# Head norm of a hybrid decoder layer: partner sums by a product with a 0/1 matrix

## The chip, the cores and the metric

The kernel runs on one core of a Trainium2 chip. The metric is the device time of one execution in microseconds (us), the median of several runs. A profile is one further execution, recorded instruction by instruction. The engines are named as the profile names them: PE is the tensor engine's matmul, PEld its weight load, DVE the vector engine, ACT the scalar engine, POOL is GpSimd, SP issues most of the DMAs.

## The reference, cut to what matters

One decoder layer over 1024 tokens and 1024 features. The input is normalised and projected to a short gated convolution group (512 columns) and to a stick-breaking attention group (8 heads of 64). Each group's output is then normalised per head of 64 features, both are joined and projected, and an MLP, a gated embedding and a last norm follow.

```python
def head_rmsnorm(y, g):
    b, s, w = y.shape
    yf = y.astype(jnp.float32).reshape(b, s, w // HEAD_DIM, HEAD_DIM)      # HEAD_DIM = 64
    yf = yf * lax.rsqrt(jnp.mean(yf * yf, axis=-1, keepdims=True) + EPS)
    return (yf.reshape(b, s, w) * g.astype(jnp.float32)).astype(y.dtype)
...
conv_out = head_rmsnorm(short_gated_conv(cb, cc, cu, conv_w[i]), g_conv_out[i])
attn = head_rmsnorm(attn.transpose(0, 2, 1, 3).reshape(b, s, W_ATTN), g_attn_out[i])
h = h + jnp.concatenate([conv_out, attn], axis=-1) @ w_out[i]
```

## The kernel before

Features lie on the 128 partitions and tokens along the free dimension, so a tile of the head norm holds two heads of 64 partitions over 1024 tokens. There are eight such tiles: four of the convolution (numbers 0 to 3, one per `conv_tile`) and four of the attention (4 to 7, one per pair of heads). A tile is worked in halves of 512 tokens.

For one half `head_norm` takes the squares on ACT (line 486), transposes them in 32x32 blocks on DVE (487) and sums 32 features at a time (489). That leaves `hpart`, 128 partitions by 16: partition quadrant q holds the sums of feature block q. A head is two neighbouring blocks, so four small copies bring each quadrant the sums of its neighbour (493), one operation adds them and the epsilon (495), and POOL raises the 16 columns to the power -0.5 (497). One slot later DVE spreads the result back over the features by another transpose (500) and multiplies the half by it and by the gain (501).

Projections, convolution and attention run interleaved between about 105 and 457 us. The order on PE there is written out by hand; the other engines' orders are planned by the scheduler from a simulated timeline. `attention_slots` counts slots. In a slot PE gets, in this order: the value products of an older chunk (`back_values`, line 645, tile `ps_av`), the transposes of a younger one (`back_transposes`, line 615, into a bank of tag `tr`), then whatever deferred work is due (`run_deferred`), then the score products of a new piece (line 586, tile `ps_z`), and last eight or so products of the projections as filler (line 158, tile `ps_mm`), taken from `fillers`. The transposed banks are emptied by an ACT copy (620) and a DVE subtraction (621); the value products use the result two slots after the transposes. Tag `tr` has two banks, taken in turn.

`head_norm` is a generator that is handed to `defer`. It starts at once; a `yield n` puts the rest off by n slots:

```python
def defer(g):
    deferred.append([slot[0] + next(g), g])
...
            elif hd == 1 and c == 1:
                defer(head_norm(y, G_ATTN + pr, 4 + pr, (0,)))
```

A convolution tile is handed over with both halves, `(0, 1)`, at the end of `conv_tile`; an attention tile half by half, as its value products end (c is the chunk of 256 tokens, hd the head). Until now no part of `head_norm` runs on PE. The squares and transposes live in a unit of group `C`, of which there are two; `conv_tile` holds one of them for its first products.

`normed` collects the finished tiles; `out_first` and the output projection's second half need them.

Of the kernel before, what the change touches and what calls it, by code (L numbers as in the profile page):

```python
# [9 lines left out]
F32 = mybir.dt.float32  # L10
F32R = mybir.dt.float32r
AF = mybir.ActivationFunctionType
ALU = mybir.AluOpType

P = 128
S = 1024
D = 1024
KT = D // P
HB = 512
NH = S // HB  # L20
EPS = 1e-6
LAG = 2
LAG_V = 2
LAG_S = 1
LAG_N = 2
QUOTA = 8.0
QUOTA_LAST = 7.4
N_WARM = 10
# [33 lines left out]
def hybrid_layer_kernel(ctx: ExitStack, tc: tile.TileContext, x, p, g_mix, w_in, conv_w, g_conv_out,  # L62
                        g_attn_out, w_out, g_mlp, w_up, w_down, g_ple, w_ple_gate, w_ple_proj,
                        g_final, out):
    nc = tc.nc
    x, p, w_in, conv_w, w_out, w_up, w_down, w_gate, w_proj, out = (
        x[0], p[0, 0], w_in[0], conv_w[0], w_out[0], w_up[0], w_down[0], w_ple_gate[0], w_ple_proj[0], out[0])

    const = ctx.enter_context(tc.tile_pool(name="const", bufs=1))
    small = ctx.enter_context(tc.tile_pool(name="small", bufs=4))  # L70
# [3 lines left out]
    U = Units(upool, {"A": 16, "VY": 10, "QK": 9, "T": 9, "W": 5, "C": 2, "E": 3})  # L74
    PS_BUFS = {"mm": 2, "z": 2, "tr": 2, "av": 2}

    def bank(tag):
        return psum.tile([P, HB], F32, name="ps_" + tag, tag=tag, bufs=PS_BUFS[tag])

    ident = const.tile([P, P], F32, name="ident")  # L80
# [10 lines left out]
                            base=0, channel_multiplier=-1)  # L91
    mhalf = const.tile([P, 16], F32, name="mhalf")
    nc.vector.memset(mhalf, -0.5)

    G_CONV, G_ATTN, CW = 0, 4, 8
    gc = const.tile([P, 20], F32, name="gc")
# [48 lines left out]
    def act_units(group):  # L145
        hi = [U.get(group, F32R, (P, 2, HB)) for _ in range(4)]
        lo = [U.get(group, F32R, (P, 2, HB)) for _ in range(4)]
        return hi, lo
# [184 lines left out]
    a, b = act_units("A")  # L333
# [12 lines left out]
    for k in range(4):  # L346
        a, b = U.get("T", F32R, (P, 2, HB)), U.get("W", F32R, (P, 2, HB))
# [47 lines left out]
    class Stream:  # L395
# [17 lines left out]
        def next(self):  # L413
            self._split()
            return self.ready.popleft()
# [59 lines left out]
    def head_norm(y, gcol, which, halves):  # L475

        for h in halves:  # L480
            while not U.free_q["C"]:
                yield 1
            sl = slice(h * HB, (h + 1) * HB)
            su = U.get("C", F32)
            sq, sqT = su[0][:, 0:HB], su[0][:, HB:S]
            nc.scalar.activation(sq, y[:, sl], AF.Square, scale=0.125)
            nc.vector.transpose(sqT, sq)
            part = small.tile([P, 16], F32, name="hpart")
            nc.vector.reduce_sum(out=part, in_=sqT.rearrange("p (b j) -> p b j", j=32), axis=mybir.AxisListType.X)
            other = small.tile([P, 16], F32, name="hother")  # L490
            for q in range(4):
                o = q ^ 1
                nc.vector.tensor_copy(out=other[32 * q:32 * q + 32], in_=part[32 * o:32 * o + 32])
            ms = small.tile([P, 16], F32, name="hms")
            nc.vector.scalar_tensor_tensor(out=ms, in0=part, scalar=EPS, in1=other, op0=ALU.add, op1=ALU.add)
            rs = small.tile([P, 16], F32, name="hrs")
            nc.gpsimd.tensor_tensor(out=rs, in0=ms, in1=mhalf, op=ALU.pow)
            if LAG_S:
                yield LAG_S
            nc.vector.transpose(sq, rs.unsqueeze(2).broadcast_to([P, 16, 32]))  # L500
            nc.vector.scalar_tensor_tensor(out=y[:, sl], in0=y[:, sl], scalar=gc[:, gcol:gcol + 1], in1=sq,  # L501
                                           op0=ALU.mult, op1=ALU.mult)
            U.put(su)
        yield LAG_N
        if halves[-1] == NH - 1:
            normed.add(which)

    def conv_tile(j, between=None):
# [29 lines left out]
        for h in range(NH):  # L538
# [4 lines left out]
            if h == 0 and between:  # L543
                between()
        stream.done(w2)
        defer(head_norm(y[0], G_CONV + j, j, (0, 1)))


# [6 lines left out]
    def run_deferred(everything=False):  # L555
        for d in list(deferred):
            while d in deferred and (everything or d[0] <= slot[0]):
                due = next(d[1], None)
                if due is None:
                    deferred.remove(d)  # L560
                else:
                    d[0] = slot[0] + due
# [64 lines left out]
    def back_values(ch, jp, aT2):  # L627
# [20 lines left out]
        if diag:  # L648
            y = Y[4 + pr][0]
            own = slice(hd * 64, hd * 64 + 64)  # L650
            oth = slice(64 - hd * 64, 128 - hd * 64)
            yc = y[own, c * 256:(c + 1) * 256]
            nc.scalar.copy(out=yc, in_=av[oth])
            nc.vector.tensor_tensor(out=yc, in0=av[own], in1=yc, op=ALU.add)
            if hd == 1 and c == 3:
                for u in V[pr]:
                    U.put(u)
                defer(head_norm(y, G_ATTN + pr, 4 + pr, (1,)))
            elif hd == 1 and c == 1:
                defer(head_norm(y, G_ATTN + pr, 4 + pr, (0,)))  # L660
# [4 lines left out]
    def attention_slots():  # L665

        def fronts():
            for pr in range(4):  # L670
                while pr not in qk_ready:
                    yield -1
                for hd in range(2):
                    for c in range(4):
                        ch = {"pr": pr, "hd": hd, "c": c}
                        for views, units in attend_front(pr, hd, c):
                            ch["views"], ch["units"] = views, units
                            yield pr
                        for jp in range(c + 1):
                            backq.append((slot[0] + LAG, ch, jp))  # L680
                    Q, K = QK[pr]
                    U.put(Q[hd])
                    for u in K[hd]:
                        U.put(u)

        fr = fronts()
        live = True
        while live or backq or pend:
            slot[0] += 1
            narrow = iter(())  # L690
            while pend and pend[0][0] <= slot[0]:
                for _ in narrow:
                    pass
                narrow = back_values(*pend.popleft()[1:])
                next(narrow, None)
            if backq and backq[0][0] <= slot[0]:
                _, ch, jp = backq.popleft()
                pend.append((slot[0] + LAG_V, ch, jp, back_transposes(ch, jp, narrow)))
            for _ in narrow:
                pass  # L700
            run_deferred()
            if live and len(U.free_q["T"]) >= 3:
                live = next(fr, None) is not None
            yield
# [72 lines left out]
    with tc.manual_schedule(engines={mybir.EngineType.PE}):  # L777
# [4 lines left out]
        for _ in attention_slots():  # L782
            credit += QUOTA if len(normed) < 6 else QUOTA_LAST
            while credit > 0:
                n = next(fill, None)
# [9 lines left out]
        for n in fill:  # L795
            slot[0] += (n or 3) / QUOTA
            run_deferred()
# [515 lines left out]
    with tc.manual_schedule(engines={mybir.EngineType.PE, mybir.EngineType.DVE, mybir.EngineType.Activation,  # L1313
# [107 lines left out]
        n = NP_ - 1  # L1421
# [231 lines left out]
```

## Time and profile before

| what | value |
|---|---|
| median of 3 runs | 1263.84 us (1262.51 to 1264.11) |
| profiled execution, its own time | 1267.23 us |
| span of the profile, first to last instruction | 1265.5 us |
| busy: PE / PEld | 1213.4 / 1004.0 us |
| busy: DVE / ACT / POOL | 963.0 / 628.5 / 236.4 us |
| mean granted TensorE clock | 0.986 of full speed |

Busy time is the sum of an engine's instructions. Matmuls are pipelined and their ends are modelled, so PE at 96% of the span is close to always occupied, but that alone does not say that it runs at its peak. The shares are means over stages with different limits; the head norm lies in one of them only, the stage from about 140 to 470 us.

### The profile page before, as it was taken

The numbers are of one execution on the slowest core, as the hardware profiler recorded it, in microseconds if no ns is written. First come the engines' busy times: TensorE is split into PE (matmuls) and PEld (weight loads), VectorE is DVE, ScalarE is ACT, GpSimd is POOL, SyncE is SP. The second block draws the span as 40 slices with busy tenths as digits, with TensorE's granted clock in tenths as the row PEclk, the third lists the DMA queues.
The fourth block names the chain that finished last, engine by engine and source line by source line (L and its number), as shares of the span: only waits on it lengthen the run. The fifth ranks groups of instructions, "written<-read, shape, count | busy, mean of one in ns | idle before, by whom it ended". The sixth has DMA issues, their size and how long they took to land.

```text
span 1265.5 us, 15613 instructions
## 1 busy us (share of the span) xinstructions
PE 1213.4 (96%) x5629; PEld 1004.0 (79%) x5629; DVE 963.0 (76%) x1367; ACT 628.5 (50%) x1049; POOL 236.4 (19%) x248
## 2 busy tenths in 40 slices
PE   8999999999998999899999999987899999999997
PEld 6788888878877788678888888865788888887786
DVE  3656898989989976678666766665889888886774
ACT  5445465555565432456545545563344444435543
POOL 3302544545448531000000000000000000002121
PEclk9999999999998999899999999989999999999899
DMA  9711011111122325124677776799787876567432
GB/s 361 221 34 44 28 31 34 35 34 34 34 67 89 128 81 203 66 92 164 231 271 251 262 276 249 276 302 325 243 258 228 264 239 214 190 207 229 134 101 99
DMA packets 152229, 209.71 MB, mean 166 GB/s; under 512 B 8004, under 2 KB 111448, under 8 KB 152152
## 3 DMA queue, kind: packets, MB, share of 16 engines
q1 hardware_dynamic: 151608, 207.67, 49.0%
q8 instruction: 44, 0.72, 0.2%
q10 hardware_dynamic: 544, 1.05, 0.2%
q14 instruction: 33, 0.27, 0.1%
HBM read 141.58 MB, written 67.11 MB: 165 GB/s over the span
## 4 chain that ended last, share of the span: by engine, by line
PE 51%; DVE 4%; DMA 3%; ACT 1%; issue 1%; SPq 0%; POOL 0%; POOLq 0%; DVEq 0%; ACTq 0%
PE ps_mm L1016 13%; PE ps_z L1016 12%; PE ps_av L1016 12%; PE ps_tr L1016 7%; PE ps_z L158 2%; PE ps_tr L158 2%; PE ps_mm L158 2%; PE ps_av L158 2%; DMA u<-hs_d 1%; DMA u<-h_d 1%; DVE u L1279 1%; DVE u L908 1%; DVE u L839 1%; DMA n_d<-u 1%; DVE u L842 1%
## 5 line engine op out<-in xcount | busy, mean ns | idle before, releaser
L158 PE MATMUL ps_mm<-u,u 128*128 128x512 f32 (+1 forms) x1464 | 366.4, 396 | 7.1 <-ACT u L904 2.6
L158 PEld LDWEIGHTS ps_mm<-u,u 128*128 128x128 f32 x1464 | 269.8, 190 | 62.3 <-ACT u L904 3.0
L908 DVE TENSOR_TENSOR u<-u,u 128x1024 fp32r<-128x1024 f32 (+2 forms) x214 | 231.2, 1101 | 43.1 <-ACT u L904 36.4
L904 ACT CAST u<-u 128x1024 fp32r<-128x1024 f32 (+2 forms) x214 | 195.0, 952 | 91.3 <-DVE u L842 20.4
L1016 PE MATMUL ps_z<-u,u 128*128 128x512 f32 x768 | 194.5, 396 | 14.4 <-DVE u L908 6.5
L1016 PE MATMUL ps_mm<-u,u 128*128 128x512 f32 x768 | 191.4, 391 | 6.5 <-DVE u L839 5.8
L1016 PE MATMUL ps_av<-u,u 128*128 128x512 f32 x744 | 186.1, 392 | 1.4 <-DVE u L908 1.4
L1016 PEld LDWEIGHTS ps_z<-u,u 128*128 128x128 f32 x768 | 145.9, 191 | 48.5 <-DVE u L908 8.3
L1016 PEld LDWEIGHTS ps_mm<-u,u 128*128 128x128 f32 x768 | 144.6, 189 | 38.2 <-DVE u L839 7.1
L1016 PEld LDWEIGHTS ps_av<-u,u 128*128 128x128 f32 x744 | 140.3, 189 | 31.8 <-DVE u L908 2.1
L123 POOL TENSOR_SCALAR me<-ms 128x1 f32<-128x1 f32 x24 | 10.3, 430 | 705.0 <-DVE u L839 619.6
L839 DVE TENSOR_TENSOR u<-ps_av,u 128x512 f32<-128x512 f32 x94 | 64.7, 689 | 81.8 <-PE ps_av L1016 48.1
L1016 PE MATMUL ps_tr<-u,u 128*128 128x512 f32 x408 | 102.0, 394 | 0.0
L1016 PEld LDWEIGHTS ps_tr<-u,u 128*128 128x128 f32 x408 | 77.6, 190 | 16.4
L603 POOL TENSOR_TENSOR u<-u,u 128x383 f32<-128x383 f32 (+5 forms) x72 | 72.7, 1012 | 94.4 <-DVE u L601 50.3
L842 DVE TENSOR_TENSOR u<-u,u 128x512 f32<-128x512 f32 (+1 forms) x120 | 84.2, 723 | 1.7
L620 ACT CAST u<-ps_tr 128x512 fp32r<-128x512 f32 (+1 forms) x80 | 43.5, 544 | 60.8 <-PE ps_tr L615 60.3
L645 PEld LDWEIGHTS ps_av<-u,u 128*128 128x128 f32 x320 | 50.2, 189 | 15.3 <-DVE u L621 9.0
L621 DVE TENSOR_TENSOR u<-ps_tr,u 128x512 fp32r<-128x512 f32 (+1 forms) x80 | 50.5, 632 | 14.8 <-ACT u L620 13.8
L596 DVE TENSOR_TENSOR_SCAN u<-u,floor 128x384 f32<-128x384 f32 (+2 forms) x64 | 58.4, 914 | 3.7 <-ACT u L588 3.6
L113 ACT CAST u<-u 128x1024 fp32r<-128x1024 f32 x42 | 43.9, 1054 | 33.9 <-DVE u L501 9.8
L645 PE MATMUL ps_av<-u,u 128*128 128x256 f32 (+1 forms) x320 | 52.9, 281 | 6.2 <-DVE u L621 6.1
(133 smaller groups left out, 1523.4 us busy)
## 6 DMA issues: line engine op xcount, KB each, us to landing
u<-in_w_down SPq DMA_DIRECT2D x56, 512.0 KB, 5.5
u<-hs_d SPq DMA_DIRECT2D x64, 448.0 KB, 5.8
hs_d<-u SPq DMA_DIRECT2D x48, 512.0 KB, 2.8
u<-in_w_up SPq DMA_DIRECT2D x32, 512.0 KB, 5.9
ws_d<-u SPq DMA_DIRECT2D x32, 512.0 KB, 2.8
u<-ws_d SPq DMA_DIRECT2D x32, 512.0 KB, 6.4
u<-in_w_in SPq DMA_DIRECT2D x24, 512.0 KB, 4.1
u<-in_x SPq DMA_DIRECT2D x16, 512.0 KB, 8.1
```

The costliest lines, as they stand in the source:

```text
L113: nc.scalar.copy(out=hi, in_=raw)
L158: nc.tensor.matmul(ps, a, b, start=(i == 0), stop=(i == n - 1))
L596: nc.vector.tensor_tensor_scan(out=rev, data0=rev, data1=floor[:, HB - (n - s0):][:, ::-1], initial=1.0, op0=ALU.mult, op1=ALU.max)
L603: (nc.vector if s0 > 0 and pr < 3 else nc.gpsimd).tensor_tensor(out=beta[:, s0:e], in0=beta[:, s0:e], in1=keep[:, s0 + 1:e + 1], op=ALU.mult)
L620: nc.scalar.copy(out=ah[:, :w], in_=tp[:, :w])
L621: nc.vector.tensor_tensor(out=al[:, :w], in0=tp[:, :w], in1=f32(ah[:, :w]), op=ALU.subtract)
L645: nc.tensor.matmul(av[:, t0:256], v, part[:, c0:c0 + 256 - t0], start=(j == 0 and part is ah), stop=(j == n - 1 and part is al))
L839: (eng or nc.vector).tensor_tensor(out=out, in0=a, in1=b, op=ALU.add)
L842: (eng or nc.vector).tensor_tensor(out=out, in0=a, in1=b, op=ALU.subtract)
L904: nc.scalar.copy(out=box["o"][0], in_=src())
L908: nc.vector.tensor_tensor(out=b, in0=src(), in1=f32(a), op=ALU.subtract)
L1016: nc.tensor.matmul(ps, a, b, start=(fresh and i == 0), stop=(i == n - 1), skip_group_check=not fresh)
```

## The change

The four small copies and the operation behind them go. A constant 128x128 matrix `neighbours` is made at the start: the identity, and ones that join each quadrant of 32 partitions with its partner. A product on PE with this matrix gives each partition the sum of both blocks of its head; the result lies in a bank of tag `tr`, from which DVE adds the epsilon. For that, `head_norm` gets one more wait of `LAG_M` = 2 slots, between the block sums and the product. Both halves of a convolution tile are summed first and then share the product, the addition and the later waits; the power stays at 16 columns an instruction. The `C` unit is given back over the waits and taken anew.

```diff
+LAG_M = 2
...
+    neighbours = const.tile([P, P], F32, name="neighbours")
+    nc.vector.tensor_copy(out=neighbours, in_=ident)
+    for q in range(4):
+        o = q ^ 1
+        nc.vector.tensor_copy(out=neighbours[32 * q:32 * q + 32, 32 * o:32 * o + 32],
+                              in_=ident[32 * q:32 * q + 32, 32 * q:32 * q + 32])
...
-        for h in halves:
-            while not U.free_q["C"]:
-                yield 1
+        while not U.free_q["C"]:
+            yield 1
+        n = 16 * len(halves)
+        su = U.get("C", F32)
+        sq, sqT = su[0][:, 0:HB], su[0][:, HB:S]
+        part = small.tile([P, 32], F32, name="hpart")[:, 0:n]
+        for i, h in enumerate(halves):
+            nc.scalar.activation(sq, y[:, h * HB:(h + 1) * HB], AF.Square, scale=0.125)
+            nc.vector.transpose(sqT, sq)
+            nc.vector.reduce_sum(out=part[:, 16 * i:16 * i + 16], in_=sqT.rearrange("p (b j) -> p b j", j=32),
+                                 axis=mybir.AxisListType.X)
+        U.put(su)
+        yield LAG_M
+        both = bank("tr")[:, 0:n]
+        nc.tensor.matmul(both, neighbours, part, start=True, stop=True)
+        ms = small.tile([P, 32], F32, name="hms")[:, 0:n]
+        nc.vector.tensor_scalar(out=ms, in0=both, scalar1=EPS, scalar2=None, op0=ALU.add)
+        rs = small.tile([P, 32], F32, name="hrs")[:, 0:n]
+        for i in range(len(halves)):
+            nc.gpsimd.tensor_tensor(out=rs[:, 16 * i:16 * i + 16], in0=ms[:, 16 * i:16 * i + 16], in1=mhalf, op=ALU.pow)
+        yield LAG_S
+        while not U.free_q["C"]:
+            yield 1
+        su = U.get("C", F32)
+        for i, h in enumerate(halves):
             sl = slice(h * HB, (h + 1) * HB)
-            su = U.get("C", F32)
-            sq, sqT = su[0][:, 0:HB], su[0][:, HB:S]
-            nc.scalar.activation(sq, y[:, sl], AF.Square, scale=0.125)
-            nc.vector.transpose(sqT, sq)
-            part = small.tile([P, 16], F32, name="hpart")
-            nc.vector.reduce_sum(out=part, in_=sqT.rearrange("p (b j) -> p b j", j=32), axis=mybir.AxisListType.X)
-            other = small.tile([P, 16], F32, name="hother")
-            for q in range(4):
-                o = q ^ 1
-                nc.vector.tensor_copy(out=other[32 * q:32 * q + 32], in_=part[32 * o:32 * o + 32])
-            ms = small.tile([P, 16], F32, name="hms")
-            nc.vector.scalar_tensor_tensor(out=ms, in0=part, scalar=EPS, in1=other, op0=ALU.add, op1=ALU.add)
-            rs = small.tile([P, 16], F32, name="hrs")
-            nc.gpsimd.tensor_tensor(out=rs, in0=ms, in1=mhalf, op=ALU.pow)
-            if LAG_S:
-                yield LAG_S
-            nc.vector.transpose(sq, rs.unsqueeze(2).broadcast_to([P, 16, 32]))
+            sq = su[0][:, sl] if len(halves) > 1 else su[0][:, 0:HB]
+            nc.vector.transpose(sq, rs[:, 16 * i:16 * i + 16].unsqueeze(2).broadcast_to([P, 16, 32]))
             nc.vector.scalar_tensor_tensor(out=y[:, sl], in0=y[:, sl], scalar=gc[:, gcol:gcol + 1], in1=sq,
                                            op0=ALU.mult, op1=ALU.mult)
-            U.put(su)
+        U.put(su)
         yield LAG_N
```

## Rows read from the trace of the kernel before

**Rows 1.** Stages: busy us (instructions) of PE, PEld, DVE, ACT, POOL; granted clock; DMA.
```profile
200.00:250.00 50.00, 50.00 (x275) 42.96 (x274) 45.96 (x75) 27.28 (x59) 28.20 (x25) 1.00 0.11 32
...
400.00:440.00 40.00, 36.98 (x183) 30.60 (x184) 39.46 (x59) 22.59 (x42) 25.37 (x23) 0.92 0.35 125
```

**Rows 2.** Waits of PE, 140 to 480 us: total us, times, longest.
```profile
PE ps_av L645 <- DVE u L621: 6.1, 8, 1.2
...
PE ps_tr L615 <- POOL u L603: 3.6, 2, 3.4
...
PE ps_mm L158 <- DVE u L114: 0.8, 1, 0.8
```

**Rows 3.** Groups by line and shape, 140 to 480 us: busy us, mean ns; idle before.
```profile
L497 POOL TENSOR_TENSOR hrs<-hms,mhalf 128x16 f32<-128x16 f32 x16 | 50.5, 3155 | 30.7 <-DVE hms L495 30.0 <-PE ps_av L645 0.7
...
L615 PEld LDWEIGHTS ps_tr<-ident,u 128*128 128x128 f32 x267 | 32.9, 142 | 9.7 <-POOL u L603 5.0 <-issue 0.2
...
L493 DVE COPY hother<-hpart 32x16 f32<-32x16 f32 x64 | 17.8, 278 | 1.1
...
L495 DVE SCALAR_TENSOR_TENSOR hms<-hpart,hother 128x16 f32<-128x16 f32 x16 | 2.6, 166 | 0.2
```

**Rows 4.** Timeline of PE, start: start us, us, instruction, count.
```profile
1.41 4.63 PE L84 MATMUL ps_warm<-ident 128*128 128x128 f32 x20 [1.41 <-POOL ident masks.py:199]
```

**Rows 5.** Timeline of PE, transposes at eight places between 176 and 434 us.
```profile
176.08 0.60 PE L615 MATMUL ps_tr<-ident,u 128*128 128x128 f32 x4
...
260.12 0.60 PE L615 MATMUL ps_tr<-ident,u 128*128 128x128 f32 x4
...
263.12 0.49 PE L615 MATMUL ps_tr<-ident,u 128*128 128x128 f32 x3
...
321.96 0.49 PE L615 MATMUL ps_tr<-ident,u 128*128 128x128 f32 x3
...
343.58 0.60 PE L615 MATMUL ps_tr<-ident,u 128*128 128x128 f32 x4
...
346.58 0.49 PE L615 MATMUL ps_tr<-ident,u 128*128 128x128 f32 x3
...
400.90 0.90 PE L615 MATMUL ps_tr<-ident,u 128*128 128x128 f32 x3 [3.39 <-POOL u L603]
...
433.70 0.60 PE L615 MATMUL ps_tr<-ident,u 128*128 128x128 f32 x4
```

**Rows 6.** Timeline of DVE at and behind the same places.
```profile
179.89 0.66 DVE L489 TENSOR_REDUCE hpart<-u 128x16 f32<-128x512 f32 x1
...
261.28 0.69 DVE L621 TENSOR_TENSOR u<-ps_tr,u 128x512 fp32r<-128x512 f32 x1
...
266.08 0.69 DVE L621 TENSOR_TENSOR u<-ps_tr,u 128x512 fp32r<-128x512 f32 x1
...
320.61 0.71 DVE L500 STREAM_TRANSPOSE u<-hrs 128x512 f32<-128x512 f32 x1 [1.24 <-POOL hrs L497]
...
323.71 0.65 DVE L621 TENSOR_TENSOR u<-ps_tr,u 128x512 fp32r<-128x512 f32 x1
...
345.38 0.69 DVE L621 TENSOR_TENSOR u<-ps_tr,u 128x512 fp32r<-128x512 f32 x1
346.10 0.70 DVE L493 COPY hother<-hpart 32x16 f32<-32x16 f32 x4
...
350.17 0.69 DVE L621 TENSOR_TENSOR u<-ps_tr,u 128x512 fp32r<-128x512 f32 x1
...
402.83 3.80 DVE L493 COPY hother<-hpart 32x16 f32<-32x16 f32 x4
...
436.25 0.68 DVE L489 TENSOR_REDUCE hpart<-u 128x16 f32<-128x512 f32 x1
```

**Rows 7.** Timeline of DVE, its first subtraction.
```profile
6.81 1.22 DVE L114 TENSOR_TENSOR u<-u,u 128x1024 fp32r<-128x1024 f32 x1 [5.33 <-ACT u L113]
```

**Rows 8.** Stage of 5 us behind the longest wait of PE.
```profile
400.00:405.00 5.00, 4.10 (x12) 3.41 (x13) 4.92 (x7) 3.76 (x6) 5.00 (x3) 0.50 0.36 114
```

## The prediction

> **What bounds the kernel now.** First the table of stages. The head norm lies in the interleaved stage of projections, convolution and attention, and there PE is busy without a gap in the stretch from 200 to 250 us, while DVE is at 92%. Only between 400 and 440 us does DVE lead, with 39.46 of 40 us, and PE falls back to 36.98 [rows 1]. So PE sets the pace and DVE follows a little behind it: an instruction less on DVE is worth something only where PE waits for DVE, and an instruction more on PE costs its full time.
>
> Then the waits of PE in that stage. Value products wait 6.1 us in 8 places for the subtraction that empties the transposed bank, transposes wait 3.6 us for POOL, and filler products wait 0.8 us for DVE [rows 2]. The sum, 10.5 us of 340, is all that a relieved DVE and POOL could give here; the 3.6 us belong to POOL's share of the beta products, which the change leaves alone, so 6.9 us are within its reach.
>
> Last the timelines of PE and DVE at the places where the new product will stand in PE's order, to see how far DVE is behind PE there.
>
> **The change, part by part.**
>
> *Removed from DVE.* 64 copies with 17.8 us and 16 additions with 2.6 us in all [rows 3]. A set of four copies takes 0.70 us at its usual pace, but 3.80 us at 402.83 [rows 6], so in the one stretch where DVE leads they are dear. In exchange 12 additions from PSUM come in; at 0.17 us each, as the old ones, they are 2 us (bound above: 0.69 us each as the bank-emptying subtractions of rows 6, 8 us). DVE is relieved by some 16 us, 10 at least. What that is worth is capped by the 6.9 us above.
>
> *Added to PE.* Four products for the convolution and eight for the attention halves, 12 in all. The warm-up products at the start show the kind (both operands plain f32): 10 calls are 20 records, so one call is two passes, and 20 records take 4.63 us, 0.23 us each [rows 4]. That is 128 columns; ours have 16 or 32, so the weight load sets the pace, and the transposes' load of the same 128x128 f32 takes 0.142 us [rows 3]. Bounds: 2 x 0.142 and 2 x 0.23 us, times 12, 3.4 to 5.6 us. I take 0.30 us each, near the lower end because the columns are few: 3.6 us, in full on PE.
>
> *The wait of the new product.* PE works in the written order, so the product holds up everything behind it: the score products of that slot, the filler and the next slot's value products. It waits for two things, the block sums from DVE and its bank of tag `tr`, which the subtraction behind the transposes of one slot earlier must have emptied. It stands two slots behind the end of the tile's value products, behind the transposes of its slot. Four halves, the first of each attention tile, fall where DVE is far behind:
> - At 176.08 the transposes end at 176.68; the block sums are there at 179.89 + 0.66 = 180.55 [rows 5, 6]. Wait 3.87 us.
> - At 260.12 they end at 260.72; the bank is free at 261.28 + 0.69 = 261.97. Wait 1.25 us.
> - At 343.58 they end at 344.18; the bank is free at 345.38 + 0.69 = 346.07. Wait 1.89 us.
> - At 433.70 they end at 434.30; the sums are there at 436.25 + 0.68 = 436.93. Wait 2.63 us.
>
> Sum 9.64 us. For a convolution tile I take the one of 321.96 us: the transposes end at 322.45 and the bank is free at 323.71 + 0.65 = 324.36, a wait of 1.91 us as things stand. But the transpose of the first half's factors, 0.71 us behind a wait of 1.24 us for POOL [rows 6], now comes later than all this, and 1.95 us less before the subtraction leave nothing. Bounds 0 to 1.9 us for each of four tiles; I take 0. The other four attention halves find sums and bank ready within some tenths; with the convolution tiles I put down 0.1 us for each of these eight, 0.8 us.
>
> *The next transposes.* The product takes one bank of two out of turn, so the transposes behind it need the bank of the slot before and not of two before. At 263.12 they would start, late by 0.30 + 1.25, at 264.67, and need the subtraction that ends at 266.08 + 0.69 = 266.77, or 265.90 without copies and addition (0.87 us): 1.23 us. At 346.58, late by 0.30 + 1.89, at 348.77, against 350.17 + 0.69 - 0.87 = 349.99: 1.22 us. Together 2.45 us; bound below 0, if DVE's order there changes. The Trainium skill (Perfetto Trace Analysis, section Matmuls) asks that independent groups of products rotate through different PSUM banks, so that one is emptied while the next is computed. By that rule alone the new product, which breaks the turn of two banks, speaks against the change; the two places agree with it.
>
> *Given back.* Where PE has waited for the new product, DVE has caught up, and the old waits for the subtraction are gone: the 6.1 us of rows 2 lie mostly right behind these places, and I count them as gone whole. The filler's wait of 0.8 us lies in the stretch with the dear copies, and I count it as gone too: 6.9 us back.
>
> *At no cost.* The five copies that make the matrix lie at the start, where DVE waits 5.33 us for its first subtraction [rows 7] (cover gone, five times the 0.17 us of a copy, 0.9 us). The power stays 16 columns an instruction, about 3 us [rows 3]; for a convolution tile two now stand back to back, 6 us of POOL, with the beta products of the attention queued behind them. A slot is some 3 us (from 260.12 to 263.12 in rows 5), and these are needed two slots, 6 us, later; where that does not do, PE waits up to 3 us. DVE's transpose of the factors could also come up to 3 us early and stand. That is inside the bound of 1.9 us for each convolution tile or just over it. The longer way of a tile (five slots for four, or for three) is covered: of the last tile only the output projection's second half has need, and its first half stands before that in PE's order as filler.
>
> *Sum:* 3.6 + 9.64 + 0.8 + 2.45 - 6.9 = 9.6 us slower. The profiled execution took 1267.23 us itself (span 1265.5), 3.4 us over the median of the runs; the sum is made in its trace: 1276.8 for such a one, 1263.84 + 9.6 = 1273.4 us for the median.
>
> **The rivals.**
>
> *Faster, DVE sums first.* The planner sets DVE's order anew. If it lets the transposes and sums of the head norm go ahead of the scans, the product never waits. Then 3.6 is paid and 6.9 comes back: -3.3 us, 1260.5 us. For it: DVE has 16 us less to do. Against it: nothing tells the planner that PE waits for this, and the rows show DVE 4 us late with the same work. It decides as long as all waits of the product and the next transposes stay under 3.3 us.
>
> *One wait for another.* The four waits halve (4.8 us) and the next transposes find their bank: 3.6 + 4.8 + 0 - 6.9 = +1.5 us, 1265.3 us. For it: each wait of the product lets DVE catch up. Against it: no value product waited longer than 1.2 us before [rows 2], and the product alone would wait 3.87 us at 176 us.
>
> *Forecast plus the clock.* The longest wait of PE in this stage, 3.39 us at 400.90, stands just before 5 us with a granted clock of 0.50, which is 1.2 GHz [rows 5, 8]: (1 - 0.50) x 5 = 2.5 us lost. The wait of 3.87 us at 176 us is as long and could bring the same: +12.1 us, 1275.9 us. For it, that row; against it, one case is all there is, and the other waits of rows 2 are too short to show where it begins. The Trainium skill (TensorE: Matmul & The Clock Gate, section HAM oscillation) says that PE's clock is halved after it has been idle, and that short bursts between waits then run cold. By that rule this is the likely end of the wait of 3.87 us; the one long wait in the trace agrees.
>
> **How the numbers follow.** Forecast 0.45, clock 0.18, one wait for another 0.17, faster 0.20. A measurement here cannot tell less than 0.2% (2.5 us) from no change: the third case is "same", the first two are slower, 0.63. The likeliest is 1273.4 us. The range goes down to 1260 us, the faster case, and up by the dearer product (+2.0) and four convolution waits of 1.9 us less the 0.4 counted (+7.2) to 1282.6 us; 1260 to 1282 us leaves out about a tenth on either side. The forecast's own range is 1267 to 1282 us.
>
> **What would show it.** Right: products of line `neighbours` on PE in pairs of records of 0.15 us, 24 in all; a wait of PE of some 3 to 4 us before the first one behind 176 us, 1 to 3 us at the other three tiles; fewer and shorter waits of the value products for the subtraction; DVE's busy time down by 10 to 16 us with a longer span. Wrong: the new product hardly waits, since the sums come two slots earlier than PE's order asks; or PE gains more than 6.9 us elsewhere, for instance at the wait for POOL at 400 us, because the planned orders of POOL and DVE shift.

## The result, and the profile after

The changed kernel takes 1273.38 us in the median (1270.29 to 1275.75, 4 runs), the kernel before 1263.97 us beside it (1262.51 to 1266.47, 4 runs). The ratio is 1.0065 with a 95% interval of 1.005 to 1.0079: slower by 9.4 us, as forecast (9.6 us), inside the range of 1260 to 1282 us. That the sum is right does not say that its terms are; this is looked at below.

The stages that answer to [rows 1], after the change (busy us and instructions of PE, PEld, DVE, ACT, POOL; granted clock; DMA):

```profile
200.00:250.00 50.00, 49.90 (x272) 42.67 (x272) 38.60 (x57) 26.68 (x57) 24.66 (x25) 1.00 0.11 32
400.00:440.00 40.00, 31.77 (x154) 26.76 (x153) 32.51 (x39) 19.43 (x37) 27.28 (x21) 0.87 0.40 132
```

DVE has its relief: 948.4 us busy in all for 963.0, 14.6 us less, inside the 10 to 16 us of the forecast. In the first stretch it is busy 38.60 us for 45.96, in the second 32.51 for 39.46 (the work of a stretch is not quite the same, since the changed kernel runs some us late). PE has nothing of it: in the second stretch it does 31.77 us of work for 36.98.

All waits of PE from 140 to 480 us, to be held against [rows 2] (total us, times, longest):

```profile
PE ps_tr L504 <- DVE hpart L499: 6.3, 2, 4.3
PE ps_tr L632 <- POOL u L620: 6.2, 1, 6.2
PE ps_tr L504 <- DVE u L638: 4.6, 3, 1.5
```

Line 504 is the new product, 632 the transposes (615 before), 638 the subtraction that empties their bank (621 before). The waits of the value products and of the filler are gone, 6.9 us of them in [rows 2]. In their place stand 10.9 us at the product, 6.3 for the block sums and 4.6 for the bank, and the wait of the transposes for POOL has grown from 3.6 to 6.2 us.

PE's timeline where the product waits (start us, us, instruction, count, idle before and what ended it):

```profile
177.37 0.60 PE L632 MATMUL ps_tr<-ident,u 128*128 128x128 f32 x4
182.24 0.37 PE L504 MATMUL ps_tr<-hpart,neighbours 128*128 128x16 f32 x2 [4.26 <-DVE hpart L499]
...
268.91 0.40 PE L504 MATMUL ps_tr<-hpart,neighbours 128*128 128x16 f32 x2 [1.53 <-DVE u L638]
...
352.38 0.40 PE L504 MATMUL ps_tr<-hpart,neighbours 128*128 128x16 f32 x2 [1.54 <-DVE u L638]
...
425.40 0.61 PE L504 MATMUL ps_tr<-hpart,neighbours 128*128 128x32 f32 x2 [2.08 <-DVE hpart L499]
...
446.67 0.39 PE L504 MATMUL ps_tr<-hpart,neighbours 128*128 128x16 f32 x2 [1.54 <-DVE u L638]
```

These are the four places of [rows 5], shifted by what was lost ahead of them, and one convolution tile (425.40, 32 columns). Where the product does not wait it is cheap. Two neighbouring slots without and with it:

```profile
244.91 0.49 PE L632 MATMUL ps_tr<-ident,u 128*128 128x128 f32 x3
245.16 0.71 PE L603 MATMUL ps_z<-u,u 128*128 128x512 f32 x2
...
248.24 0.49 PE L632 MATMUL ps_tr<-ident,u 128*128 128x128 f32 x3
248.56 0.31 PE L504 MATMUL ps_tr<-hpart,neighbours 128*128 128x32 f32 x2
248.71 0.48 PE L603 MATMUL ps_z<-u,u 128*128 128x256 f32 x2
```

From the start of the transposes to that of the scores it is 0.25 us without and 0.47 us with the product: 0.22 us, and 2.6 us for twelve if all cost the same (an estimate from this one pair).

Last the clock behind the longest wait (columns as in the stages):

```profile
183.00:186.40 3.40, 3.40 (x13) 3.01 (x12) 0.63 (x3) 1.16 (x2) 2.90 (x1) 0.50 0.02 5
186.40:190.00 3.60, 3.60 (x18) 3.00 (x18) 3.52 (x6) 2.74 (x5) 0.55 (x1) 1.00 0.00 0
```

PE is busy all through the first stretch, but at 0.50 of its clock, 1.2 GHz: 13 matmuls in 3.4 us, then 18 in 3.6 us. Half of 3.4 us, 1.7 us, is lost there besides the wait, and the same once more behind the wait at 425.40 us:

```profile
425.30:428.70 3.40, 3.30 (x10) 2.85 (x11) 1.30 (x3) 0.66 (x2) 2.40 (x2) 0.50 0.31 124
```

Behind the wait for POOL both kernels run at 0.50 for about 6.8 us (before 399.6 to 406.3 us, after 408.3 to 415.0 us), so that loss of 3.4 us is in both.

### The profile page after: what moved, and what is told of

Its sections match the earlier page's. It is cut to its first block, busy times and chain, and to the rows that moved or that the text cites. A ratio compares the mean times of both kernels' runs of the same rounds, so it can differ in the third digit from the quotient of the medians.

```text
span 1272.6 us, 15596 instructions
## 1 busy us (share of the span) xinstructions
PE 1215.0 (95%) x5653; PEld 1008.2 (79%) x5653; DVE 948.4 (75%) x1304; ACT 629.7 (49%) x1049; POOL 239.5 (19%) x248
## 3 DMA queue, kind: packets, MB, share of 16 engines
q10 hardware_dynamic: 544, 1.05, 0.2%
## 4 chain that ended last, share of the span: by engine, by line
PE 48%; DVE 4%; DMA 4%; ACT 2%; issue 1%; SPq 0%; POOL 0%; DVEq 0%; POOLq 0%; ACTq 0%
PE ps_z L1033 12%; PE ps_mm L1033 12%; PE ps_av L1033 12%; PE ps_tr L1033 7%; DMA u<-h_d 2%; PE ps_z L167 1%; PE ps_tr L167 1%; PE ps_mm L167 1%; PE ps_av L167 1%; DVE u L1296 1%; DMA n_d<-u 1%; DVE u L856 1%; DVE u L925 1%; DMA u<-hs_d 1%; DVE u L859 1%
## 5 line engine op out<-in xcount | busy, mean ns | idle before, releaser
L1033 PEld LDWEIGHTS ps_av<-u,u 128*128 128x128 f32 x744 | 140.3, 189 | 33.0 <-DVE u L925 2.1
L620 POOL TENSOR_TENSOR u<-u,u 128x383 f32<-128x383 f32 (+5 forms) x72 | 76.2, 1059 | 89.5 <-DVE u L618 40.6
L610 POOL TENSOR_SCALAR_AFFINE_SELECT u<-u 128x128 f32<-128x128 f32 x64 | 36.6, 572 | 124.2 <-ACT u L606 124.1
L605 ACT ACTIVATE u<-ps_z 128x384 f32<-128x384 f32 (+3 forms) x96 | 47.4, 494 | 20.4 <-PE ps_z L603 19.2
```

Of the source, the lines that this page charges most:

```text
L605: nc.scalar.activation(keep[:, s0:s1], z[:, :s1 - s0], AF.Sigmoid, scale=-1.0)
L620: (nc.vector if s0 > 0 and pr < 3 else nc.gpsimd).tensor_tensor(out=beta[:, s0:e], in0=beta[:, s0:e], in1=keep[:, s0 + 1:e + 1], op=ALU.mult)
L1033: nc.tensor.matmul(ps, a, b, start=(fresh and i == 0), stop=(i == n - 1), skip_group_check=not fresh)
```

## The experiments

The theory (A): PE waits at the new product, because two slots behind the tile's last value product neither the block sums nor the bank are sure to be there, and PE works in the written order. Rival B: the bank, taken out of its turn, is the cause, not the sums. Rival C: the time is lost through the planner's new order on POOL and DVE around the last convolution tile. Each run is compared with the kernel before on the same chip; the ratio is that of its runs to those of the kernel before, with a 95% interval.

### The product alone: kept copies, a product that nobody reads

In the kernel before. The result does not depend on the added lines.

```diff
-        yield LAG_N
+        yield 1
+        nc.tensor.matmul(bank("tr")[:, 0:16], neighbours, part, start=True, stop=True)
+        yield 1
```

> The kernel before with the copies kept, and twelve products with the 0/1 matrix added whose results nobody reads, each two slots behind its block sums (of a convolution tile the second half only) and in a bank of the transposes' tag. It shows the price of the product and its waits alone. Theory A: 12 products of 0.23 us and waits like those of the changed kernel, less what is given back: 1270 to 1277 us. Rival B: the same. Rival C: the product is cheap without the new order, 1265 to 1269 us.

1272.2 us, ratio 1.0053 (1.0035 to 1.0071). PE's waits in it, 140 to 480 us; 512 is the product, 496 the block sums, 630 the subtraction, 624 the transposes:

```profile
PE ps_tr L512 <- DVE hpart L496: 6.2, 3, 3.8
PE ps_tr L512 <- DVE u L630: 3.3, 2, 1.7
PE ps_tr L624 <- POOL u L612: 3.2, 1, 3.2
PE ps_mm L165 <- DVE u L121: 0.8, 1, 0.8
PE ps_av L654 <- DVE u L630: 0.7, 3, 0.3
```

The product by itself brings most of the loss, with the same kind of waits, 9.5 us, and takes most of the value products' old waits away, 0.7 for 6.1 us. The wait for POOL is as before, and so is the filler's. Rival C is not the main cause. The 2.4 us that are left of the 9.4 lie within the two intervals, and no run assigns them.

### The relief alone: no copies and no product

In the changed kernel; a head is normalised by 32 features in place of 64.

```diff
-        both = bank("tr")[:, 0:n]
-        nc.tensor.matmul(both, neighbours, part, start=True, stop=True)
...
-        nc.vector.tensor_scalar(out=ms, in0=both, scalar1=EPS, scalar2=None, op0=ALU.add)
+        nc.vector.tensor_scalar(out=ms, in0=part, scalar1=EPS, scalar2=None, op0=ALU.add)
```

> The changed kernel without the product: epsilon is added to the block sums themselves, so a head is normalised by 32 features and not by 64; DVE has the relief, PE nothing more to do. It shows what the relief alone is worth. Theory A: 6.9 us at most, the waits of PE that DVE causes, 1257 to 1262 us. Rival B: the same. Rival C: the new order on POOL and DVE costs some 3 to 5 us without the product as well, 1264 to 1270 us.

1265.99 us, ratio 1.0007 (0.9993 to 1.0022): DVE's relief, with nothing paid on PE, is worth nothing that can be measured. Theory A's 1257 to 1262 us was wrong. PE's waits in this run:

```profile
PE ps_tr L630 <- POOL u L618: 7.1, 3, 6.1
PE ps_av L660 <- DVE u L636: 4.5, 5, 1.3
```

The value products wait 4.5 us for 6.1 before, the filler no more; but the transposes wait 7.1 us for POOL where they waited 3.6. The timeline of POOL shows why. First the run with the unread product, where the order is the old one (612 is the beta product, 121 a split of a tile in `prepare_first`), then this run (618 and 123):

```profile
405.13 1.16 POOL L612 TENSOR_TENSOR u<-u,u 128x512 f32<-128x512 f32 x1
406.26 5.17 POOL L121 TENSOR_TENSOR u<-u,u 128x1024 fp32r<-128x1024 f32 x2
```

```profile
399.51 2.45 POOL L123 TENSOR_TENSOR u<-u,u 128x1024 fp32r<-128x1024 f32 x1
401.92 1.47 POOL L618 TENSOR_TENSOR u<-u,u 128x512 f32<-128x512 f32 x1
```

Two splits stand ahead of the beta product that the transposes wait for in either order; now a third, of 2.45 us, does as well. So there is a part of rival C: 2.7 us more of waiting (6.1 for 3.4 us at the longest), in the changed kernel too, where POOL has the same order (the split at 405.52, the beta product at 407.93 us). Whether it costs time is another matter: this run, which has the wait, is no slower than the kernel before.

### Shared small operations alone: copies in place of the product

```diff
-        both = bank("tr")[:, 0:n]
-        nc.tensor.matmul(both, neighbours, part, start=True, stop=True)
+        other = small.tile([P, 32], F32, name="hother")[:, 0:n]
+        for q in range(4):
+            o = q ^ 1
+            nc.vector.tensor_copy(out=other[32 * q:32 * q + 32], in_=part[32 * o:32 * o + 32])
...
-        nc.vector.tensor_scalar(out=ms, in0=both, scalar1=EPS, scalar2=None, op0=ALU.add)
+        nc.vector.scalar_tensor_tensor(out=ms, in0=part, scalar=EPS, in1=other, op0=ALU.add, op1=ALU.add)
```

> The changed kernel with copies in place of the product: both halves of a convolution tile share the small operations, the waits of 2 and 1 slots stand, nothing new on PE. It shows the other half of the change. Theory A: without the product no wait and no price on PE; DVE saves only 4 of 16 sets of copies: 1262 to 1267 us, like the kernel before. If the order on POOL turns with the sharing and the later wait, and not with the missing copies, the wait for POOL near 400 us is 6 us here too: 1266 to 1270 us.

1265.12 us, ratio 1.0008 (0.9997 to 1.0019), no change. PE waits 6.1 us for POOL here as well:

```profile
PE ps_tr L634 <- POOL u L622: 7.5, 4, 6.1
```

So this wait grows with the sharing and the later waits of the norm; the missing copies are not needed for it. The 1266 to 1270 us that were expected with such a wait did not come. This half of the change costs nothing and brings nothing.

### The product later: LAG_M 4

```diff
-LAG_M = 2
+LAG_M = 4
```

> The changed kernel with the product two slots later (LAG_M 4 for 2), all else the same. Theory A, PE waits at the product because the block sums and the bank come too late: two slots are some 6 us, more than the longest wait of 4.26 us, so the waits at the product go; the 11 us come off and some of the old waits of the value products (6.1 us) return: 1263 to 1268 us. Rival B, the product takes its bank out of turn and the waits are for the bank: the place in the turn stays, so at most half goes: 1268 to 1271 us. Rival C, the time is lost through the planner's new order on POOL and DVE around the last convolution tile (a wait of 6.15 us for POOL): no change, 1271 to 1275 us.

1268.11 us, ratio 1.0021 (1.0007 to 1.0036): just over what theory A gave and at the lower end of what rival B gave, so the time does not choose between them. All waits of PE from 140 to 480 us:

```profile
PE ps_tr L632 <- POOL u L620: 10.5, 5, 8.6
PE ps_av L662 <- DVE u L638: 2.1, 3, 0.8
PE ps_mm L167 <- DVE u L123: 0.6, 1, 0.6
```

No wait at the product is left, where rival B left half of them, and the value products wait 2.1 us for 6.1 before. This does not refute B, though: two slots later the product also meets another turn of the banks, as is seen below. The long wait that is left is for POOL: now all four splits stand ahead of the beta product,

```profile
392.25 12.87 POOL L123 TENSOR_TENSOR u<-u,u 128x1024 fp32r<-128x1024 f32 x4 [0.58 <-ACT u L122]
...
405.46 1.74 POOL L620 TENSOR_TENSOR u<-u,u 128x512 f32<-128x512 f32 x1
```

and PE waits 8.6 us for it.

### Another bank, at two slots

```diff
-        both = bank("tr")[:, 0:n]
+        both = bank("av")[:, 0:n]
```

> The changed kernel with the product in a bank of the value products' tag instead of the transposes'. The longest waits behind the change are one for the block sums (4.26 us) and five for a bank (1.5 to 2.1 us). Theory A: the sums are late anyway, the product waits little less; time within 3 us of the changed kernel, 1270 to 1275 us. Rival B, the bank: five waits of together some 7 us go, 1265 to 1268 us. Rival C: no change.

1271.63 us, ratio 1.0055 (1.0034 to 1.0075). The waits at the product are all for the sums now, 8.3 us for the 10.9 us in the changed kernel:

```profile
PE ps_av L504 <- DVE hpart L499: 8.3, 5, 4.2
```

At two slots the sums are late by themselves; the bank adds 2.6 us of waiting, and the times do not tell the two kernels apart. (The expectation counted five waits for a bank; the list of the changed kernel has three, 4.6 us in all, so B should have said some 1269 us, still under what was measured.) As the main cause rival B falls for this place of the product. It comes back at another one, below.

### The splits off POOL

The four splits of `prepare_first` use POOL. First those of the two Y tiles, then those of the weights too, go to DVE:

```diff
-            first_w2.append(split_unit(load_rows(w_out, f, "W"), "A", nc.gpsimd))
-            first_y2.append(split_unit(Y[f], "A", nc.gpsimd))
+            first_w2.append(split_unit(load_rows(w_out, f, "W"), "A"))
+            first_y2.append(split_unit(Y[f], "A"))
```

With the Y tiles on DVE, in the changed kernel, with LAG_M 4, and in the kernel before:

> The changed kernel with the two splits of Y tiles on DVE. If the wait of 6.15 us for POOL at 409 us is a part of the loss (2.8 us over the 3.39 us before): that wait goes, and with it some half clock, 1262 to 1269 us; the waits at the product stay (4 us at 182 us, 1.5 us at 269, 352 and 447 us). If it is chance order: 1271 to 1275 us.

> LAG_M 4, and the two splits of Y tiles in prepare_first (each up to 3.4 us on POOL) go from POOL to DVE, which has room since the relief. In the run with LAG_M 4 alone four splits (12.87 us on POOL) stood ahead of the beta product that PE's transposes waited 8.57 us for at 407 us, with 10 us at half clock behind it. Theory A with the part of rival C that is now seen (the relief lets the planner put the splits ahead of that beta product): the wait and most of the half clock go, 1268 - 6 to 1268 - 12 us, that is 1256 to 1262 us, faster than the kernel before. Rival: DVE takes the two splits (some 3 us with what they shut out) and PE waits there instead: 1264 to 1268 us.

> Control: the kernel before with the two splits of Y tiles on DVE. There DVE is full from 400 to 440 us (39.46 of 40), so it should gain less than the others: the wait of 3.39 us for POOL goes, waits for DVE of 1 to 3 us come: 1259 to 1265 us. If it gains as much as with LAG_M 4 (6 us or more), the gain has nothing to do with the relief.

The changed kernel: 1270.89 us, ratio 1.0051 (1.0032 to 1.007). The wait for POOL falls from 6.15 to 2.96 us, but the time gains only 2.5 us against the result, inside both spreads; it lies just under the range for chance order, so this run does not show that the wait for POOL is a part of the loss. With LAG_M 4: 1263.28 us, ratio 0.9988 (0.9979 to 0.9997), between the ranges of theory and rival; the longest wait for POOL is 4.4 us, for 8.6. The kernel before: 1265.3 us, ratio 1.0005 (0.9994 to 1.0016), no gain, a little over the range expected; its wait for POOL did not go and is 3.4 us as before.

With all four on DVE:

> LAG_M 4 and all four splits of prepare_first on DVE, none on POOL. With two of them moved a wait of 4.36 us for POOL at 403 us and 6.8 us at half clock were left. If those two splits on POOL make that wait, it goes: 1263.3 - 4 to 1263.3 - 7 us, 1256 to 1260 us. Rival: DVE, 47.5 of 50 us busy there with two splits, is full and PE waits for it instead: 1262 to 1266 us.

> Control: the kernel before with all four splits on DVE. Its DVE is full from 400 to 440 us, so it gains less than the relieved kernel: 1261 to 1266 us. If it comes out like the run with LAG_M 4, the relief is worth nothing here either.

LAG_M 4: 1261.44 us, ratio 0.997 (0.9957 to 0.9982), faster than both kernels, between theory and rival. The kernel before: 1263.79 us, ratio 0.9986 (0.9975 to 0.9997). The two intervals overlap a little, but these two were run side by side on one chip, and their own runs can be compared: the means differ by 2.4 us (95% interval 0.8 to 4.0 us). The pair with only the Y tiles moved says the same, 2.3 us (1.4 to 3.2 us). So with the product at a better place the change does bring some 2.4 us, about 0.2%, over the kernel before with the same splits moved. PE's waits with LAG_M 4 and no split on POOL:

```profile
PE ps_tr L632 <- POOL u L620: 4.4, 4, 2.8
PE ps_av L662 <- DVE u L638: 2.7, 4, 0.8
PE ps_mm L167 <- DVE u L123: 2.2, 2, 1.6
```

9.3 us in all, not far from the 10.5 us of [rows 2]: most of what was freed on DVE was not what PE waited for.

### Three slots, and three slots with another bank

The same kernel with `LAG_M = 3`:

> The same with the product three slots behind its sums. Theory A: at two slots the longest wait is 4.2 us and the others 0.8 to 2 us, a slot is some 3 us: one wait of 1 to 1.5 us is left at the first attention tile, so at most 2 us over the run with LAG_M 4. If the time with LAG_M 4 comes from the later end of the norm, 3 is better than 4.

1277.38 us, ratio 1.0095 (1.0076 to 1.0114), 16 us slower than with 4, and slower than the kernels with 2 (1273.38 and 1270.89 us, which still have splits on POOL). The expectation, that a later product waits less, was wrong. Its waits at the product, and one of them on the timelines of PE and then DVE:

```profile
PE ps_tr L504 <- DVE u L638: 7.8, 3, 3.0
PE ps_tr L504 <- DVE hpart L499: 3.3, 1, 3.3
```

```profile
266.50 0.60 PE L632 MATMUL ps_tr<-ident,u 128*128 128x128 f32 x4
...
269.97 0.49 PE L632 MATMUL ps_tr<-ident,u 128*128 128x128 f32 x3
273.45 0.40 PE L504 MATMUL ps_tr<-hpart,neighbours 128*128 128x16 f32 x2 [2.99 <-DVE u L638]
```

```profile
268.05 0.69 DVE L499 TENSOR_REDUCE hpart<-u 128x16 f32<-128x512 f32 x1
...
272.70 0.69 DVE L638 TENSOR_TENSOR u<-ps_tr,u 128x512 fp32r<-128x512 f32 x1
```

The sums were ready at 268.74, the product could have run at 270.5. But it stands right behind the transposes of 269.97, so its bank is that of the transposes of 266.50, and DVE empties it only at 273.39. At four slots this tile's product falls into a slot without transposes, behind value products, and runs at once (PE's timeline of that run):

```profile
267.91 0.62 PE L662 MATMUL ps_av<-u,u 128*128 128x256 f32 x3 [0.84 <-DVE u L638]
268.37 0.29 PE L504 MATMUL ps_tr<-hpart,neighbours 128*128 128x16 f32 x2
```

To tell whether it is the bank, the same with `bank("av")`:

> The run with the product three slots behind its sums and no split on POOL, with the product in a bank of the value products' tag. In that run (1277 us) three waits of 1.8 to 3.0 us were for the bank, 273.45 us for instance 0.5 us behind the transposes of the slot, and one of 3.3 us for the sums. If the bank out of its turn is the cause: these three waits go or halve, 1277.4 - 6 to 1277.4 - 14 us, 1263 to 1271 us. If it is DVE's delay whatever the bank: 1273 to 1278 us.

1264.8 us, ratio 1.0002 (0.999 to 1.0015): 12.6 us less from the bank alone (on another chip, where the kernel before differs by 0.5 us). Of the waits at the product one is left, for the sums:

```profile
PE ps_av L504 <- DVE hpart L499: 3.2, 1, 3.2
```

So rival B is right at three slots, and theory A in its first form, sums too late, is right for the greater part of the waits at two. Both are waits at the product for DVE.

## Why the prediction was right, step by step

**What bounds the kernel.** Right: a product of 0.22 us on PE and its waits cost 7 us with the copies kept, and the relief of DVE, alone, is worth nothing. Even the cap of 6.9 us was high: without copies and without a product the waits for DVE fall by 2.4 us only (4.5 for 6.9), and the wait for POOL is 3.5 us longer (7.1 for 3.6), with no change of the time. Only with the product two slots later and splits moved off POOL does the change gain, some 2.4 us over the kernel before with the same splits moved. The size of the relief was summed wrongly: its own rows give 17.8 + 2.6 - 2 = 18.4 us, 12.4 with the dearer additions, not 16 and 10; measured over the whole execution it is 14.6 us.

**The price of the product.** Forecast 3.6 us, measured some 2.6 us. The lower bound from the transposes' weight load (3.4 us) was itself too high. The group of the loads (busy us, mean ns) shows 24 of them:

```profile
L504 PEld LDWEIGHTS ps_tr<-hpart,neighbours 128*128 128x128 f32 x24 | 3.9, 199 | 12.5 <-issue 6.8 <-DVE u L638 5.3 <-PE ps_tr L632 0.3
```

Each takes longer than the 0.142 us that I had put down, but two of them and their products take only 0.22 us of PE's time: they lie beside the work before.

**Its waits at four places.** Forecast 3.87, 1.25, 1.89 and 2.63 us, measured 4.26, 1.53, 1.54 and 1.54: 9.64 against 8.87 us, each for the reason named (sums at the first, bank at the second and third) except the last, which waited for the bank and not for the sums. That the product's place in PE's order can be held against DVE's old timeline was the step that carried the forecast, and the unread product and LAG_M 4 show it: waits with it, none when it stands two slots later. (The rival in which these waits halve did not come; its other half, that the next transposes find their bank, did.)

What the waits cost in the end differs from place to place, which the forecast's one sum hides. The same transposes of the two traces tell how late PE is. Before the first wait it is 1.05 us (152.52 for 151.47 us), behind it 6.20 us (185.56 for 179.36). The second wait brings that to 8.66 us (271.78 for 263.12), but 7 us later it is back at 6.44 (279.04 for 272.60); the third brings it to 8.68 (355.26 for 346.58), then 5.81 (362.52 for 356.71). So what these two cost comes back at once from the waits that the value products no longer have, while the first, with half clock behind it, stays: the largest single part of the loss.

**The eight others.** Forecast 0.8 us, measured 2.1: one convolution tile at 425.40 us waited 2.08 us, just over the bound of 1.9 us, where I had taken 0; and it waited for its sums, where the bound was for the bank.

**The next transposes.** Wrong: forecast 2.45 us, measured 0. The list of waits after the change has none of transposes for line 638. I had taken it that they need the bank of the slot before, but they start while that bank is still waiting for DVE (PE, then DVE):

```profile
271.78 0.49 PE L632 MATMUL ps_tr<-ident,u 128*128 128x128 f32 x3
```

```profile
272.10 0.69 DVE L638 TENSOR_TENSOR u<-ps_tr,u 128x512 fp32r<-128x512 f32 x1
```

This subtraction of 512 columns belongs to the four transposes of one slot earlier, at 266.78 us, and ends 1.0 us after the next ones have begun. Of the tag's two banks that leaves the product's own, which DVE's small addition (line 506) had read by 270.05 us. It is the same at the third place (transposes at 355.26 us, the subtraction of the slot before at 355.57). So behind the product the banks were not taken strictly in turn, and the product gave its bank back early. The Trainium skill's rule on rotating PSUM banks (Perfetto Trace Analysis, section Matmuls) holds here all the same, at the product itself: with three slots the same product is 12.6 us cheaper in a bank that is not shared with the transposes.

**What is given back.** Right in size: 6.9 us forecast, and the waits of value products and filler are gone whole. The unread product shows it for the value products: with all copies kept they wait 0.7 us. They are given back by the product's waits, as written, and for the lesser part by the relief (the run without copies and product has 4.5 us of 6.1 left). The filler's wait of 0.8 us stands in the run with the unread product and is gone in the two without product, with the copies and without; so that part comes of the norm's new order and not of the product.

**What the sum left out.** Two things. The wait for POOL grew by 2.6 us (6.2 for 3.6), because the planner put one more split ahead of a beta product; the forecast named POOL's order only as something that could go wrong the other way. That this growth costs time is not shown: the two kernels without the product have it and take no longer than the kernel before. And the clock: the rival "forecast plus the clock" happened in the profiled execution, behind the wait of 4.26 us and behind that of 2.08 us, 1.7 us each; 2.5 us had been put down, for the first alone. The profiles of the unread product, of the other bank at two slots and of the Y splits on DVE show half clock behind the first wait too. (The row that the 2.5 us came from showed 5 us; the half clock there lasts 6.8 us and costs 3.4.) The Trainium skill (TensorE: Matmul & The Clock Gate, section HAM oscillation) says that work behind a long enough idle stretch starts at half clock; the 13 matmuls in 3.4 us at a granted clock of 0.50 agree.

So the sum, with what was measured, reads 2.6 + 8.9 + 2.1 + 0 - 6.9 + 2.6 + 3.4 = 12.7 us, where the medians are 9.4 us apart and the two profiled executions, 1274.3 and 1267.23 us, 7.1 us. The terms were over- and underestimated by 1 to 3 us each and met at the right total; the mechanism is shown, the agreement to a tenth of a us is luck. Where the rest is can be followed in the two traces. Where the stage ends, the first product behind it starts at 485.23 us for 473.91, 11.3 us late. Of this 1.0 us is there at 24 us already, at the start, where the clock is at 0.50 for 6.8 us for 3.4; the copies that make the matrix are not the reason, as DVE's first subtraction starts no later (6.67 us for 6.81). So the sum stands against some 10 us, 2 to 3 us too high. Behind the stage 4.2 us come back, in stretches that the change does not touch and that differ in clock: from 1155 to 1185 us it is 0.89 before and 1.00 after, 3.3 us.

**The rival on the other side** (the planner lets the sums go first) did not come. DVE's timeline ahead of the first wait, after the change:

```profile
178.95 0.71 DVE L498 STREAM_TRANSPOSE u<-u 128x512 f32<-128x512 f32 x1
179.69 0.69 DVE L638 TENSOR_TENSOR u<-ps_tr,u 128x512 fp32r<-128x512 f32 x1
180.30 1.22 DVE L613 TENSOR_TENSOR_SCAN u<-u,floor 128x512 f32<-128x512 f32 x1
181.43 0.66 DVE L499 TENSOR_REDUCE hpart<-u 128x16 f32<-128x512 f32 x1
```

A bank's subtraction and a scan stand between the head norm's transpose and its sum, 1.8 us of the 4.26 that PE waits. The arithmetic of that rival, too, rested on the 6.9 us that the relief alone did not bring.

## What to carry to other kernels

On an engine that works in a written order, a small instruction costs less by its duration than by its place: look up, in the trace of before, when its operands and its buffer will be free at that place, and count what is queued behind it. A user that takes a buffer out of another's ring waits for whoever still holds it; give it a buffer of another ring or a slot where the ring rests. Relief of an engine that is 90% busy is worth only the waits that the bound engine has for it, and a planner that fills the freed time may put other work ahead of what is waited for; so look at the order of the third engine too.

## What the runs showed of the hardware that was not expected

A plain f32 product of 128x128 by 16 or 32 columns is two records with a weight load each; one with 32 columns took 0.22 us of PE's time between other products.

A wait well under the longest can bring the lower clock, and then the clock costs more than the wait. The stage from 140 to 480 us with four slots and with three, no split on POOL (columns as in the stages above), and the stretch behind the second 3 us wait with three:

```profile
140.00:480.00 340.00, 330.65 (x1767) 280.13 (x1766) 287.61 (x398) 188.16 (x367) 163.14 (x146) 1.00 0.18 56
```

```profile
140.00:480.00 340.00, 324.72 (x1696) 275.50 (x1695) 284.94 (x386) 183.49 (x363) 158.01 (x144) 0.96 0.16 50
...
274.80:278.20 3.40, 3.40 (x11) 2.73 (x10) 3.33 (x5) 0.72 (x2) 3.03 (x2) 0.50 0.00 0
```

The waits differ by 6.0 us (15.3 for 9.3 us), the times by 16 us. With three slots five stretches of the stage, 23.9 us together, are at 0.50, with four slots none: 11.9 us, so most of that loss is clock. The length of the wait alone does not decide: one of 2.8 us with four slots was not followed by half clock, one of 3.0 us with three slots was; in the changed kernel one of 2.08 us (at 425.40 us) was, and one of 2.06 us for the same tile, in the kernel with the Y splits on DVE, was not.
